# Grouped-query scores from stacked fp32r parts, decay tables behind the attentions, and a projection between MLA's transposes and products

## The chip, the cores and the metric

The kernel runs on one core of a Trainium2 chip. The metric is device time in microseconds of one execution; a run's time is the time of that core. The engines are named as the profile names them: PE (TensorE, the matmuls), PEld (its weight loads), DVE (VectorE), ACT (ScalarE), POOL (GpSimd) and SP (SyncE, which here issues most DMAs). fp32r is a 32-bit type that PE multiplies in one pass with shortened mantissas; the kernel splits an fp32 operand into a part hi and a part lo of that type and adds the products.

## The reference

One inference step of a two-layer trunk of width 1024 for 128 prompt tokens and 256 sample tokens. Each layer mixes tokens in four head groups (retention, hyena, windowed grouped-query attention, multi-head latent attention) that share one input and one output projection, and then runs a gated MLP with a short convolution. The sample's tokens read 128 cached context tokens. Cut to what matters here (GQA has 4 query heads on 2 key heads of 64, MLA 4 heads of 64+32):

```python
def rms_norm(x, g):
    xf = x.astype(jnp.float32)
    y = xf * lax.rsqrt(jnp.mean(xf * xf, axis=-1, keepdims=True) + EPS)
    return (y * g.astype(jnp.float32)).astype(x.dtype)
...
def window_attention(q, k, v, k_ctx, v_ctx, sink):
...
    valid = (jnp.abs(kpos - qpos) <= WINDOW) & (kpos >= 0) & (kpos < seq_len)
    scale = d ** -0.5
    s_win = jnp.einsum('bkgnqd,bknjd->bkgnqj', qb, kw).astype(jnp.float32) * scale
    s_win = jnp.where(valid, s_win, NEG_INF)
    s_ctx = jnp.einsum('bkgnqd,bkcd->bkgnqc', qb, k_ctx).astype(jnp.float32) * scale
...
    pr = jax.nn.softmax(jnp.concatenate([s_win, s_ctx, s_sink], axis=-1), axis=-1).astype(v.dtype)
...
def token_mixer(h, p, cache):
...
    proj = h @ p['w_in']
    ret_in, hy_in, gqa_in, mla_in = jnp.split(proj, [RET_IN, RET_IN + HY_IN, RET_IN + HY_IN + GQA_IN], axis=-1)
...
    y_ret, ret_state = retention_mixer(ret_in, p['ret_decay_logit'], p['ret_gn_g'], s0)
    y_hy = hyena_mixer(hy_in, p)
...
    mq = (rms_norm(q_lat, p['mla_q_norm']) @ p['mla_w_uq']).reshape(
        b, seq_len, MLA_HEADS, MLA_NOPE + MLA_ROPE).transpose(0, 2, 1, 3)
...
    ckv = rms_norm(kv_lat, p['mla_kv_norm'])
    if latent:
...
        o_gqa = window_attention(apply_rope(gq, cos_g, sin_g), apply_rope(gk, cos_g, sin_g), gv,
                                 cache['gqa_k'], cache['gqa_v'], sink)
...
        o_gqa = dense_attention(gq, gk, gv, HEAD_DIM ** -0.5, sink)
...
    o_mla = dense_attention(mq, mk, mv, (MLA_NOPE + MLA_ROPE) ** -0.5, None)[:, :, 0]
...
    y = jnp.concatenate([y_ret, y_hy, y_gqa, y_mla], axis=-1) @ p['w_out']
    return y, ctx_state
...
def trunk_layer(x, mod, p, cache):
    shift1, scale1, gate1, shift2, scale2, gate2 = mod
    h = rms_norm(x, p['norm_g'][0]) * (1.0 + scale1) + shift1
    y, ctx_state = token_mixer(h, p, cache)
    x = x + gate1 * rms_norm(y, p['norm_g'][1])
    h = rms_norm(x, p['norm_g'][2]) * (1.0 + scale2) + shift2
    x = x + gate2 * rms_norm(conv_ffn(h, p), p['norm_g'][3])
    return x, ctx_state
```

## The kernel before

The tokens stand transposed, 128 features on the partitions, in 386 columns: the prompt (128), and the two halves of the sample (128 each) with gap columns. The program speaks of them as u=0, 1, 2 and of their first columns as C0 = [0, 130, 258], or T0 = [0, 128, 256] where there are no gaps. Weights come from HBM in units of 512 KB into tiles raw (DMAs of SP); ACT casts a unit into whi (L358) and DVE makes wlo (L359), in halves of 512 columns. A projection of 128 features (fmps) is 24 fp32r matmuls of 386 columns: 8 blocks of 128 input features by three products, hi x hi, hi x lo, lo x hi (mm3, L383 to L385).

The mixer phase of a layer has these parts. A block with an order written out by hand for PE, DVE, ACT and SP holds the token-major projections (tma), the k projection of GQA, MLA's rotary key, norm, transposes (ckt, qlt, krps) and up-projections (ukps, uvps, uqps), and GQA's q projection u=0. The generators mla and gqa hand over at each yield, and the block says with next(ml) and next(gq) who goes on. Behind the block a scheduler decides the order from data dependencies, its own estimates and program order; there come the rest of mla (its attention), the rest of gqa (the projection u=1, gsw with the rope, its attention), hyena's six projections, and retention's.

An attention (attend, L893 to L932) does the groups u = 1, 2, 0 in turn. For one group: four heads' scores on PE into four banks, for each a maximum on DVE (L900); negm (L905); four exponentials on ACT with their sums (L908); for GQA the sink's term (L912 to L914); rc (L916); then two rounds of: P times rc (L922), six transposes ptp on PE (L925), two copies PT (L926, DVE and ACT), the products pv (L930), and a split of the result. GQA's scores before are fp32 matmuls on 64 rows (L1058, 384 columns; for the prompt L1056, 128 columns), and a bf16 matmul adds the mask (L1060). Their operands lie in one tile gqk (k in kall, q behind it); gfm tiles of the tag w15 hold the projections until the rope (gsw on PE, L1034; products on DVE and POOL, sum on DVE, L1036 to L1039) has gone into gqk.

PSUM has eight banks: two in a pool for the tag a (fmps and a few sums), five of the tag m, one n. SBUF tags are rings: the tag w15 has 11 tiles of 128 x 386, given out in program order; GQA's three gfm tiles, the six of hyena's cv (L1078 to L1080, which free a bank of fmps) and, in layer 0, the lag table and four tabt tiles of the decay tables come from it. In layer 0 the decay tables (load_lp: L540 to L560 with a chain of small operations lgp; rettab: L563 to L577) stand in the program ahead of the attentions; those of layer 1 are made in layer 0's FFN. PE also runs the adaLN projection of layer 0 in this phase (adaps, L407, four matmuls side by side) wherever its data is there.

## Time and profile before

| | before |
|---|---|
| median of 3 runs | 1088.33 us (1086.99 to 1088.36) |
| the profiled execution | 1084.69 us, of which the span shown is 1082.9 us |
| PE busy | 1059.6 us, 98% of the span |
| DVE / ACT / POOL busy | 727.2 (67%) / 504.3 (47%) / 61.5 us (6%) |
| chain that ended last | PE 86%, DVE 8%, DMA 2%, ACT 2% |
| HBM traffic | 162 GB/s over the span |

The profile is one execution. Its times run from the start of the span; layer 0's mixer lies from about 54 to 230 us, layer 1's from about 590 to 790. In rows of the time line the columns are start, duration, engine, line, operation, output and inputs with shape and type, and the number of instructions that the row joins; a bracket tells how long the engine had been idle and who released it. A matmul's duration holds its drain too, so what one costs in a series is read from the distance of two starts.

### The profile page before, as it was taken

The page shows a single profiled execution, that of the slowest core. Times are in us where ns is not written, and L with a number is a line of the kernel's source. Part 1 is how long each engine was busy: PE and PEld are TensorE (multiplying, and loading weights), DVE is VectorE, ACT ScalarE, POOL GpSimd, SP SyncE. Part 2 cuts the span into 40 slices and gives each one's busy share as a digit, 9 for nine tenths or more (in the row PEclk, how much of TensorE's full clock was granted, in tenths as well). Part 3 has the DMA queues.
Part 4 walks back from the last instruction along what each step waited for, and adds up shares of the span by engine and source line. Part 5 has one row for each costly group of instructions (what it writes and reads, how often), then busy time and mean ns, then how long its engine had stood idle before and what let it go on. Part 6 is the DMA issues. An engine that isn't in the chain of part 4 may idle for free.

```text
span 1082.9 us, 15620 instructions
## 1 busy us (share of the span) xinstructions
PE 1059.6 (98%) x5763; PEld 894.1 (83%) x5763; DVE 727.2 (67%) x1544; ACT 504.3 (47%) x1106; POOL 61.5 (6%) x74
## 2 busy tenths in 40 slices
PE   9999999999889999999999999999999999999997
PEld 4496767768789999899996977886899999999996
DVE  5868965476789885799557577757766455545544
ACT  5754635334734344333447454552584344334333
POOL 2210000000200000000002000001020000000000
PEclk9999999999999999999999999999999999999999
DMA  9674345855576764577356522231535433443301
GB/s 345 231 278 169 118 155 178 302 168 222 180 250 201 226 215 150 159 234 221 124 169 209 179 79 77 60 97 41 217 109 191 129 117 118 136 131 122 119 19 58
DMA packets 53017, 176.05 MB, mean 163 GB/s; under 512 B 8618, under 2 KB 10538, under 8 KB 52429
## 3 DMA queue, kind: packets, MB, share of 16 engines
q1 hardware_dynamic: 49229, 171.19, 47.2%
q10 hardware_dynamic: 3712, 3.87, 1.0%
q8 instruction: 45, 0.74, 0.3%
q14 instruction: 31, 0.25, 0.1%
HBM read 169.60 MB, written 5.44 MB: 162 GB/s over the span
## 4 chain that ended last, share of the span: by engine, by line
PE 86%; DVE 8%; DMA 2%; ACT 2%; issue 1%; POOL 0%; ACTq 0%; DVEq 0%; SPq 0%; POOLq 0%
PE ups L383 5%; PE ups L385 5%; PE ups L384 5%; PE gps L383 5%; PE facc L1283 5%; PE facc L1285 5%; PE gps L385 5%; PE gps L384 5%; PE facc L1284 5%; PE fmps L383 4%; PE fmps L385 4%; PE fmps L384 4%; PE adaps L407 2%; PE acc L1283 2%; PE acc L1284 2%; PE acc L1285 2%
## 5 line engine op out<-in xcount | busy, mean ns | idle before, releaser
L359 DVE TENSOR_TENSOR wlo<-raw,whi 128x512 fp32r<-128x512 f32 (+2 forms) x388 | 254.4, 686 | 169.0 <-ACT whi L358 168.5
L358 ACT CAST whi<-raw 128x512 fp32r<-128x512 f32 (+2 forms) x388 | 221.6, 611 | 276.5 <-DMA raw<-in_wdn_dram 99.1
L1283 PE MATMUL facc<-whi,fah 128*128 128x512 f32 x264 | 105.3, 399 | 2.7 <-ACT fah L358 2.7
L1285 PE MATMUL facc<-whi,fal 128*128 128x512 f32 x264 | 104.5, 397 | 0.2 <-DVE fal L359 0.2
L1284 PE MATMUL facc<-wlo,fah 128*128 128x512 f32 x264 | 104.5, 396 | 0.0
L505 DVE SCALAR_TENSOR_TENSOR avc<-avr,cs,avc 128x1024 f32<-128x1024 f32 x56 | 70.3, 1282 | 0.3 <-DMA avr<-in_ada_dram 0.2
L383 PE MATMUL gps<-hTa,whi 128*128 128x386 f32 (+4 forms) x184 | 62.5, 340 | 0.0
L383 PE MATMUL ups<-hTb,whi 128*128 128x386 f32 (+4 forms) x184 | 61.7, 335 | 0.6 <-ACT hTb L812 0.6
L384 PE MATMUL ups<-hTb,whi 128*128 128x386 f32 (+4 forms) x184 | 61.4, 334 | 0.8 <-POOL hTb L815 0.8
L385 PE MATMUL gps<-hTa,wlo 128*128 128x386 f32 (+4 forms) x184 | 62.0, 337 | 0.0
L384 PE MATMUL gps<-hTa,whi 128*128 128x386 f32 (+4 forms) x184 | 61.8, 336 | 0.0
L383 PE MATMUL gps<-hTb,whi 128*128 128x386 f32 (+4 forms) x184 | 61.7, 335 | 0.0
L383 PE MATMUL ups<-hTa,whi 128*128 128x386 f32 (+4 forms) x184 | 61.7, 335 | 0.0
L385 PE MATMUL ups<-hTb,wlo 128*128 128x386 f32 (+4 forms) x184 | 61.5, 334 | 0.0
L385 PE MATMUL gps<-hTb,wlo 128*128 128x386 f32 (+4 forms) x184 | 61.4, 334 | 0.0
L385 PE MATMUL ups<-hTa,wlo 128*128 128x386 f32 (+4 forms) x184 | 61.4, 334 | 0.0
L384 PE MATMUL ups<-hTa,whi 128*128 128x386 f32 (+4 forms) x184 | 61.3, 333 | 0.0
L384 PE MATMUL gps<-hTb,whi 128*128 128x386 f32 (+4 forms) x184 | 61.3, 333 | 0.0
L1285 PEld LDWEIGHTS facc<-whi,fal 128*128 128x128 f32 x264 | 50.0, 189 | 13.1 <-DVE fal L359 1.3
L1283 PEld LDWEIGHTS facc<-whi,fah 128*128 128x128 f32 x264 | 50.0, 189 | 13.0 <-ACT fah L358 3.0
L1284 PEld LDWEIGHTS facc<-wlo,fah 128*128 128x128 f32 x264 | 50.0, 190 | 10.1
L1299 ACT ACTIVATE fth<-fc 128x386 f32<-128x386 f32 x44 | 23.2, 528 | 59.9 <-DVE fc L1298 59.9
(381 smaller groups left out, 2371.4 us busy)
## 6 DMA issues: line engine op xcount, KB each, us to landing
raw<-in_wup_dram SPq DMA_DIRECT2D x88, 512.0 KB
araw<-in_ada_dram SPq DMA_DIRECT2D x64, 512.0 KB
raw<-in_wdn_dram SPq DMA_DIRECT2D x44, 512.0 KB
avr<-in_ada_dram SPq DMA_DIRECT2D x32, 512.0 KB
raw<-in_win_dram SPq DMA_DIRECT2D x30, 512.0 KB
raw<-in_wout_dram SPq DMA_DIRECT2D x16, 512.0 KB
gg<-gd SPq DMA_DIRECT2D x8, 512.0 KB
raw<-in_wta_dram SPq DMA_DIRECT2D x8, 416.0 KB
```

Of the source, the lines that this page charges most:

```text
L358: S.copy(hi, src)
L359: (eng or V).tensor_tensor(out=lo, in0=src, in1=hi, op=ALU.subtract)
L383: T.matmul(out, ah, bh, start=start, stop=False)
L384: T.matmul(out, ah, bl, start=False, stop=False)
L385: T.matmul(out, al, bh, start=False, stop=stop)
L407: T.matmul(self.ps[32 * j:32 * j + 32, :], cs[:, k, :], rows[j // 2][:, 512 * (j % 2):512 * (j % 2) + 512], start=(k == self.k0), stop=(k ...
L505: V.scalar_tensor_tensor(out=acc[:, v, c], in0=raw, scalar=sc, in1=acc[:, v, c], op0=ALU.mult, op1=ALU.add)
L1283: T.matmul(acc[t][h], ah[:, cs_], wh_[:, hs], start=first, stop=False)
L1284: T.matmul(acc[t][h], ah[:, cs_], wl_[:, hs], start=False, stop=False)
L1285: T.matmul(acc[t][h], al[:, cs_], wh_[:, hs], start=False, stop=last)
L1299: S.activation(out=th, in_=c, func=ACTF.Tanh)
```

## The change

Four things are edited.

1. GQA's scores. k goes into a tile gkf (tag mq, which MLA's mq uses later), and from it into kh (hi, on both halves of the rows) and kl (lo on the rows of its own head group, zeros on the other half, set by POOL). For each query head a tile gq of the tag w15 has q's hi part in 64 rows and its lo part in the other 64. One fp32r matmul of gq with kh and one with kl, on 128 rows each, take the place of the fp32 matmul. The rope is added in place in gfm or gkf, behind gsw, which reads it. The context keys stand behind the sample's now, so vals and the mask's place change. The copies L1040 go.
2. Layer 0's decay tables: load_lp is cut into the load and lp_tables; lp_tables and retention_tables of layer 0 stand in the program behind both attentions.
3. MLA yields behind its transposes, and the block with the written order puts GQA's projection u=0 between these and the up-projections; the split of its weight is written ahead of the k projection's, in tiles of its own.
4. In the FFN, the steps of the next layer's adaLN vectors (AdaV, DVE) start at f = 3, not 1.

```diff
--- before.py
+++ after.py
@@ -536,6 +536,9 @@
             o, w = poff[name]
             return t[:, o + a:o + (w if b is None else b)]
 
+        return t, get
+
+    def lp_tables(t, get):
         fh = lpp.tile([128, NF, 4], F32, tag="ffh", name="ffh")
         V.tensor_scalar(fh.rearrange("p f t -> p (f t)"), get("ffc"), 0.5, None, ALU.mult)
 
@@ -985,6 +988,7 @@
             T.transpose(ps[0:96, o:o + 128], kr[:, t, :], ident)
         for h in range(4):
             (S.copy if h % 2 else V.tensor_copy)(mk[64:96, h, 128:512], ps[64:96, 128:512])
+        yield
         wuk, wuv = M("wuk"), M("wuv")
         wuq = M("wuq").rearrange("p (k h m) -> p k h m", k=2, h=4)
         for hp in range(2):
@@ -1020,49 +1024,61 @@
 
     def gqa(l, mx, my, M, hi, lo, tma, sink, ws):
 
-        gqk = mx.tile([128, 2048], F32, tag="gqk", name="gqk")
-        kall = gqk[:, 0:512]
-        nc.sync.dma_start(out=kall[:, 0:128], in_=A["kcT"][l])
+
+        kf = my.tile([128, 514], F32, tag="mq", name="gkf")
+        gqk = mx.tile([128, 4, 514], F32R, tag="gqk", name="gqk")
+        kh, kl = gqk[:, 0:2], gqk[:, 2:4]
+        nc.sync.dma_start(out=kf[:, 386:514], in_=A["kcT"][l])
+        halfs = [slice(0, 64), slice(64, 128)]
+        for g in range(2):
+            G.memset(kl[halfs[1 - g], g].bitcast(F32), 0.0)
         yield
-        q = gqk[:, 512:1280].rearrange("p (t c) -> p t c", t=2)
+        qs = {}
         rc, rs_ = cc("rc"), cc("rs")
         for u in (2, 0, 1):
             ps = fm_mm(ws.pop(0), hi, lo) if ws else fm_proj(l, u, hi, lo)
-            fm = mx.tile([128, TP], F32, tag="w15", name="gfm", bufs=11)
-            S.activation(out=fm, in_=ps[:, 0:TP], func=ACTF.Copy, scale=1.0 if u == 2 else 0.125)
+            fm = kf if u == 2 else mx.tile([128, TP], F32, tag="w15", name="gfm", bufs=11)
+            S.activation(out=fm[:, 0:TP], in_=ps[:, 0:TP], func=ACTF.Copy, scale=1.0 if u == 2 else 0.125)
             sw = bank("m", "gsw")
             T.matmul(sw[:, 0:256], cc("perm"), fm[:, 130:386], start=True, stop=True)
-            ds_, dp = (kall[:, 128:384], kall[:, 384:512]) if u == 2 else (q[:, u, 128:384], q[:, u, 0:128])
             tmp = my.tile([128, 256], F32, tag="k1", name="grt", bufs=2)
             V.tensor_tensor(out=tmp, in0=sw[:, 0:256], in1=rs_, op=ALU.mult)
-            G.tensor_tensor(out=ds_, in0=fm[:, 130:386], in1=rc, op=ALU.mult)
-            V.tensor_tensor(out=ds_, in0=ds_, in1=tmp, op=ALU.add)
-            V.tensor_copy(dp, fm[:, 0:128])
             if u == 2:
                 pk = bank("m", "gkt")
                 T.transpose(pk[:, 0:128], fm[:, 0:128], ident)
                 ko = my.tile([128, 128], F32, tag="ko", name="ko")
                 S.copy(ko, pk[:, 0:128])
                 nc.scalar.dma_start(out=O["o_k"][l].rearrange("g t d -> t g d"), in_=ko.rearrange("t (g d) -> t g d", g=2))
+            G.tensor_tensor(out=fm[:, 130:386], in0=fm[:, 130:386], in1=rc, op=ALU.mult)
+            V.tensor_tensor(out=fm[:, 130:386], in0=fm[:, 130:386], in1=tmp, op=ALU.add)
+            for g in range(2):
+                a, b = halfs[g], halfs[1 - g]
+                if u == 2:
+                    S.copy(kh[a, g], kf[a])
+                    V.tensor_copy(kh[b, g], kf[a])
+                    V.tensor_tensor(out=kl[a, g], in0=kf[a], in1=kh[a, g], op=ALU.subtract)
+                else:
+                    q = qs[2 * g + u] = mx.tile([128, TP], F32R, tag="w15", name=f"gq{2 * g + u}", bufs=11)
+                    S.copy(q[a], fm[a])
+                    V.tensor_tensor(out=q[b], in0=fm[a], in1=q[a], op=ALU.subtract)
             yield
         nc.scalar.dma_start(out=O["o_v"][l].rearrange("g t d -> t g d"),
                             in_=tma[:, 0, 256:384].rearrange("t (g d) -> t g d", g=2))
         vc = M("vc")
         for u in (1, 2, 0):
             def score(ps, h):
-                r = 64 * (h // 2)
-                lq = q[r:r + 64, h % 2, T0[u]:T0[u] + 128]
-                if u == 0:
-                    T.matmul(ps[:, 0:128], lq, kall[r:r + 64, 384:512], start=True, stop=True)
-                else:
-                    T.matmul(ps[:, 0:384], lq, kall[r:r + 64, 0:384], start=True, stop=False)
-                    mo = 256 if u == 1 else 128
+                q, g = qs[h][:, C0[u]:C0[u] + 128], h // 2
+                k0, n = (0, 128) if u == 0 else (130, 384)
+                T.matmul(ps[:, 0:n], q, kh[:, g, k0:k0 + n], start=True, stop=False)
+                T.matmul(ps[:, 0:n], q, kl[:, g, k0:k0 + n], start=False, stop=(u == 0))
+                if u:
+                    mo = 256 - 128 * u
                     T.matmul(ps[:, mo:mo + 128], identb, maskb[:, 128 * (u - 1):128 * u], start=False, stop=True)
             def vals(k, h):
                 g = 64 * (h // 2)
                 if u == 0:
                     return tma[:, 0, 256 + g:320 + g]
-                return vc[:, g:g + 64] if k == 0 else tma[:, k, 256 + g:320 + g]
+                return vc[:, g:g + 64] if k == 2 else tma[:, 1 + k, 256 + g:320 + g]
             attend(mx, my, score, 128 if u == 0 else 384, 1.0, sink(), vals, 4, u)
 
 
@@ -1415,23 +1431,28 @@
                 wsplit(uw[0], *us[0], 0)
                 wsplit(uw[0], *us[0], 1)
                 next(ml)
+                us.append(wparts())
+                wsplit(uw[1], *us[1], 0)
+                wsplit(uw[1], *us[1], 1)
                 next(gq)
-                us.append(wparts())
-                wsplit(uw[1], *us[0], 0)
-                wsplit(uw[1], *us[0], 1)
                 next(ml)
                 next(gq)
+                next(ml)
                 end = V.tensor_copy(zero8, zero8)
             if l == 0:
                 mkf = hm.tile([128, 256], F32, tag="hm", name="mkf")
                 nc.sync.dma_start(out=mkf, in_=A["mask"])
                 with tc.issue_after(end.ins):
                     V.tensor_copy(maskb, mkf)
-                    lps = load_lp(0)
-                    rt = retention_tables(lps[2], mx, tag="w15", bufs=11)
-            get, fh, lgt = lps
+                    lp0 = load_lp(0)
+                get = lp0[1]
+            else:
+                get, fh, lgt = lps
             run(ml)
             run(gq)
+            if l == 0:
+                _, fh, lgt = lp_tables(*lp0)
+                rt = retention_tables(lgt, mx, tag="w15", bufs=11)
             hyg = hyena(l, mx, my, get, sp, hi, lo)
             reg = retention(l, mx, M, get, rt, hi, lo, tma)
             next(hyg)
@@ -1537,7 +1558,7 @@
                 act[f] = (ah, al)
                 with late if f == 0 else nullcontext():
                     wd[f] = wunit(A["wdn"][l, f], 1024, fx, STAG)
-                if f not in (0, 4, 5):
+                if f > 2 and f not in (4, 5):
                     next(nexts, None)
                     next(nexts, None)
                 if f == NF - 1:
@@ -1546,7 +1567,7 @@
                     if f == 4:
                         sp = per.tile([128, 3, 2, 512], F32, tag="spec", name="spec")
                         nc.sync.dma_start(out=sp, in_=sd[l + 1])
-                        lps = load_lp(l + 1)
+                        lps = lp_tables(*load_lp(l + 1))
                         rt = retention_tables(lps[2], av, tag="avr", bufs=2)
             run(nexts)
             avc.__exit__(None, None, None)

```

What moves is shown here as lists of instructions in an engine's order, with the tiles' numbers (they differ between the two programs).

PE, layer 1, the end of MLA's attention (its group u=0: ptp, pv) and the start of GQA's (gsw, sc); fmps are projections. Before:

```order
L385 MATMUL fmps_6868<-hTa_5483,wlo_6863 128x386
L383 MATMUL fmps_6868<-hTb_5487,whi_6862 128x386
L930 MATMUL pv_6445<-PT_6436,mv_6172 64x128 x2
L1034 MATMUL gsw_6499<-gfm_6497,cst_80 128x256
L1058 MATMUL sc_6507<-gqk_5944 128x384
L1060 LDWEIGHTS identb_94
L1060 MATMUL sc_6507<-maskb_95,identb_94 128x128
L384 MATMUL fmps_6868<-hTb_5489,whi_6862 128x386
L385 MATMUL fmps_6868<-hTb_5487,wlo_6863 128x386
```

Now:

```order
L928 MATMUL ptp_6469<-cst0_79,P_6454 128x128
L933 MATMUL pv_6472<-PT_6463,mv_6247 64x128 x2
L928 MATMUL ptp_6479<-cst0_79,P_6455 128x128
L928 MATMUL ptp_6483<-cst0_79,P_6456 128x128
L933 MATMUL pv_6486<-PT_6477,mv_6247 64x128 x2
L1043 MATMUL gsw_6540<-gfm_6538,cst_80 128x256
L1072 MATMUL sc_6553<-gqk_5974,gq0_6233 128x384
L1073 MATMUL sc_6553<-gqk_5974,gq0_6233 128x384
L1076 LDWEIGHTS identb_94
L1076 MATMUL sc_6553<-maskb_95,identb_94 128x128
L1072 MATMUL sc_6554<-gqk_5974,gq1_6546 128x384
```

No fmps stands between MLA's prompt scores and the end of GQA's first scores now; 120 stand ahead of that place in layer 1, where 157 stood, and 120 in layer 0, where 167 stood.

ACT, layer 1, the first copy cv of a hyena projection. Before, it stands between two groups of MLA's attention (P are its exponentials):

```order
L926 COPY PT_6304<-ptp_6312 128x3x128
L358 CAST whi_6862<-raw_6860 128x512 x2
L358 CAST mix_6300<-pv_6317 128x128
L1078 ACTIVATE cv_6759<-fmps_6734,lp_3537 128x386
L908 ACTIVATE P_6342,ssum_6340<-sc_6326,negm_6339 128x384
L908 ACTIVATE P_6343,ssum_6340<-sc_6327,negm_6339 128x384
```

Now, it stands behind the last group of MLA's attention and the casts of GQA's q tiles gq1 and gq3:

```order
L929 COPY PT_6463<-ptp_6469 128x128
L358 CAST mix_6341<-pv_6472 128x128
L929 COPY PT_6477<-ptp_6483 128x128
L358 CAST mix_6341<-pv_6486 128x128
L1062 CAST gq1_6546<-gfm_6538 64x386
L1062 CAST gq3_6549<-gfm_6538 64x386
L1094 ACTIVATE cv_6817<-fmps_6792,lp_3550 128x386
L1094 ACTIVATE cv_6862<-fmps_6837,lp_3550 128x386
L911 ACTIVATE P_6578,ssum_6575<-sc_6553,negm_6574 128x384
```

The first two cv have moved from MLA's attention to behind gq3. In layer 0 the two first cv follow gq3 too.

DVE, layer 0, the softmax of GQA's first group (u=1: mxv, negm, es, ssum, rc, P). Before:

```order
L900 TENSOR_REDUCE mxv_1375<-sc_1374 128x1
L359 TENSOR_TENSOR wlo_1856<-raw_1853,whi_1855 128x512
L904 TENSOR_TENSOR mxv_1375<-mxv_1375,lp_1057 128x4
L905 TENSOR_SCALAR negm_1388<-mxv_1375 128x4
L912 TENSOR_TENSOR es_1400<-lp_1057,negm_1388 128x4
L914 TENSOR_TENSOR ssum_1389<-ssum_1389,es_1400 128x4
L916 RECIPROCAL rc_1404<-ssum_1389 128x4
L922 TENSOR_SCALAR P_1392<-P_1392,rc_1404 128x384
```

Now:

```order
L903 TENSOR_REDUCE mxv_1328<-sc_1327 128x1
L573 TENSOR_SCALAR tab_1589<-lag_1585,lgt_1559 128x384
L907 TENSOR_TENSOR mxv_1328<-mxv_1328,lp_1069 128x4
L574 TENSOR_SCALAR tabt_1590<-lag_1585,nlg_1587 128x384
L908 TENSOR_SCALAR negm_1345<-mxv_1328 128x4
L573 TENSOR_SCALAR tab_1589<-lag_1585,lgt_1559 128x384
L915 TENSOR_TENSOR es_1357<-lp_1069,negm_1345 128x4
L575 TENSOR_TENSOR tab_1589<-tab_1589,tabt_1590 128x384
L574 TENSOR_SCALAR tabt_1596<-lag_1585,nlg_1587 128x384
L573 TENSOR_SCALAR tab_1589<-lag_1585,lgt_1559 128x384
L575 TENSOR_TENSOR tab_1589<-tab_1589,tabt_1596 128x384
L574 TENSOR_SCALAR tabt_1602<-lag_1585,nlg_1587 128x384
```

Operations of the decay tables (tab, tabt) stand among those of the softmax now; the tables' chains of small operations (lgp), of both layers, stand ahead of MLA's norm in layer 0.

## Rows read from the trace of the kernel before

**Rows 1.** The profile's busy times: engine, busy us, share, instructions.

```profile
PE 1059.6 (98%) x5763; PEld 894.1 (83%) x5763; DVE 727.2 (67%) x1544; ACT 504.3 (47%) x1106; POOL 61.5 (6%) x74
```

**Rows 2.** Stretches: from:to, length, busy us (instructions) of PE, PEld, DVE, ACT, POOL; clock; DMA.

```profile
637.00:670.00 33.00, 32.95 (x211) 27.78 (x211) 24.25 (x65) 17.72 (x49) 1.15 (x2) 1.00 0.21 65
```

**Rows 3.** What PE waited for from 612 to 640: total us, times, longest.

```profile
PE ukps L992 <- ACT ckvT L975: 1.0, 1, 1.0
PE uvps L998 <- ACT mv L999: 0.7, 1, 0.7
PE uvps L998 <- ACT mk L987: 0.3, 1, 0.3
```

**Rows 4.** Time line of PE, layer 1, GQA's scores of u=1.

```profile
674.15 0.91 PE L1058 MATMUL sc<-gqk 64*128 64x384 f32 x2
...
675.15 0.91 PE L1058 MATMUL sc<-gqk 64*128 64x384 f32 x2
...
676.03 0.42 PE L385 MATMUL fmps<-hTb,wlo 128*128 128x386 f32 x1
676.29 0.34 PE L383 MATMUL fmps<-hTb,whi 128*128 128x386 f32 x1
676.47 0.35 PE L384 MATMUL fmps<-hTb,whi 128*128 128x386 f32 x1
```

**Rows 5.** Time line of PE, layer 1, GQA's scores of the prompt.

```profile
699.62 0.72 PE L1056 MATMUL sc<-gqk 64*128 64x128 f32 x8
```

**Rows 6.** Time line of PE, layer 1, MLA's u=2 and u=0, then GQA's u=1.

```profile
650.20 2.85 PE L1016 MATMUL sc<-mk,mq 96*128 96x384 f32 x8
...
657.53 0.85 PE L925 MATMUL ptp<-cst,P 128*128 128x128 f32 x6
...
662.64 1.16 PE L1016 MATMUL sc<-mk,mq 96*128 96x128 f32 x8
...
667.00 0.38 PE L925 MATMUL ptp<-cst,P 128*128 128x128 f32 x2
...
670.24 0.70 PE L1034 MATMUL gsw<-gfm,cst 128*128 128x256 f32 x2
...
680.74 0.94 PE L925 MATMUL ptp<-cst,P 128*128 128x128 f32 x6
...
682.29 0.45 PE L930 MATMUL pv<-PT,lm 128*64 128x128 f32 x4 [0.25 <-ACT PT L926]
```

**Rows 7.** Time line of DVE, layer 1, the split ahead of negm.

```profile
653.56 0.68 DVE L359 TENSOR_TENSOR wlo<-raw,whi 128x512 fp32r<-128x512 f32 x1
```

**Rows 8.** Time line of PE, layer 0, from MLA's prompt scores to GQA's u=2.

```profile
136.40 1.16 PE L1016 MATMUL sc<-mk,mq 96*128 96x128 f32 x8
...
144.19 0.70 PE L1034 MATMUL gsw<-gfm,cst 128*128 128x256 f32 x2
...
155.49 1.06 PE L407 MATMUL adaps<-araw,cs 128*32 128x512 f32 x8
...
156.77 0.82 PE L925 MATMUL ptp<-cst,P 128*128 128x128 f32 x6
...
161.35 0.91 PE L1058 MATMUL sc<-gqk 64*128 64x384 f32 x2
```

**Rows 9.** Time line of DVE, layer 0's tables, and PE's wait behind them.

```profile
109.00 0.17 DVE L558 TENSOR_SCALAR lgp<-lgp 128x12 f32<-128x12 f32 x1
...
113.25 0.41 DVE L570 TENSOR_SCALAR tab<-lag,lgt 128x384 f32<-128x384 f32 x1
113.58 0.55 DVE L572 TENSOR_TENSOR tab<-tab,tabt 128x384 f32<-128x384 f32 x1
...
119.28 0.88 PE L925 MATMUL ptp<-cst,P 128*128 128x128 f32 x6 [0.78 <-DVE P L922]
```

**Rows 10.** Stretches at the end of the span, columns as in group 2.

```profile
1076.00:1080.00 4.00, 0.00 (x0) 0.00 (x0) 2.78 (x8) 0.98 (x3) 0.00 (x0) 1.00 0.20 77
...
1081.00:1082.90 1.90, 0.00 (x0) 0.00 (x0) 0.00 (x0) 0.00 (x0) 0.00 (x0) 0.50 0.13 49
```

## The prediction, before any run of the changed kernel

> **What bounds the kernel now.** I read the page's busy times first: TensorE (PE) is busy 98% of the span [rows 1], so time can only be lost or won in what PE executes and in the gaps between. Then the table by stretches: the stretch of layer 1 that holds MLA's attention has 32.95 us of PE work in 33.00 us [rows 2]. It is that full because the scheduler puts hyena projections (fmps, matmuls of 386 columns) between an attention's scores, its transposes (ptp) and its products (pv); the softmax on DVE and ACT runs beneath them. Then the waits: PE's real gaps in this part of layer 1 are three, before MLA's up-projections: 1.0, 0.7 and 0.3 us [rows 3]. So the question for each edit is not how long an operation takes on DVE or ACT, but how much PE work is left to stand beneath the chain it belongs to.
>
> **Scores.** A windowed GQA head costs 1.00 us: 674.15 to 675.15, score and mask [rows 4]. In fp32r a matmul of 386 columns follows the one before after 0.18 us, and the first one behind a bf16 mask after 0.26 us [rows 4]. A new head is an entry of 0.26, one more at 0.18 and the mask at some 0.05, so 0.5 us: four heads gain 2.0 us, and there are two such groups in each layer (u=1, u=2). The trace shows no fp32r matmul of a 64-row pair stacked to 128; bounds are 0.9 us a head (were each as slow as half an fp32 pair) and 0.4, and I take 0.5, since rows and columns are those of the fmps. The prompt's scores (u=0) were eight entries of fp32 on 128 columns in 0.72 us [rows 5]; eight fp32r ones cost at most 8 x 0.18 = 1.4 and, with a third of the columns, at least 0.5: +0.3 for each layer, between -0.2 and +0.7.
>
> **Where the fill goes.** This term decides. The four q tiles take places in the 11-buffer tag w15 that hyena's cv tiles also use, in program order: two gfm and four gq per layer, where three gfm stood. The order lists show what follows: ACT's first cv copy stands behind the casts of gq1 and gq3, and these need the last gsw, which waits behind the whole MLA attention. The projections' PSUM pool has two banks; until cv is copied out, two hyena units fill them and PE can start no third. So exactly 120 fmps (three GQA and two hyena units) stand before GQA's first score, in either layer; before, 167 stood there in layer 0 and 157 in layer 1. PE executes in order, so the stretches behind the 120th are as long as their dependency chains. The displaced fmps themselves run later at the same 0.18 us. I count, for each stretch, its length less its fill, before and after.
>
> Layer 1, first score of MLA's u=2 to first of u=0: 650.20 to 662.64 is 12.44 us [rows 6] with 33 fmps (5.9), so 6.6 uncovered. After: 11 fmps (2.0) are left. The softmax from first score to first ptp took 7.33, of which one split of a weight stood in DVE's queue right ahead of negm (0.6, [rows 7]): 6.7; two rounds of ptp, copy and pv without fill take some 4.3, worked out from ptp to pv below. 11.0 - 2.0 = 9.0: **+2.4**.
>
> MLA's u=0 to gsw: 662.64 to 670.24 is 7.60 [rows 6] with 29 fmps (5.2), 2.4 uncovered. After: no fill. Scores to ptp took 4.36 [rows 6], less some 0.4 of copies and order; two rounds on 128 columns are 2.0. 5.9 uncovered: **+3.5**.
>
> gsw to the end of the scores: 670.24 to 676.03, 5.8 with 7 fmps (1.2). After: gq1 needs gsw, two rope products, the add, a cast and a subtraction, some 2.9 us, with a reduce possibly in between, then three heads at 0.5: 4.5 to 5.3 without fill. **+0.4**; the first group's 2.0 us are spent here.
>
> GQA's u=1 softmax: 676.03 to 680.74, 4.7 [rows 4, 6], was covered by 26 fmps. After 23 are left and the scores come twice as fast as the reduces follow: **+1.0**. From ptp to pv it is 1.55 us with 0.25 idle in spite of two fmps [rows 6]; three remain. u=2 keeps 29 fmps over the same chain, so its scores' gain counts: **-1.8**. The three waits of [rows 3] go, because the u=0 projection now stands between the transposes and the up-projections and gives ACT's copies seven us: **-2.0**. With u=0's scores (+0.3) and some more changes between fp32 and fp32r (0.08 each, +0.3), layer 1 loses **4.1 us**.
>
> Layer 0: MLA's u=2 keeps its adaLN groups (adaps, 1.0 us a group, [rows 8]) as fill: 0. u=0 to gsw, 136.40 to 144.19 [rows 8], loses 23 fmps and comes down to the same 5.9 with one group and a piece: 2.7 uncovered before, 4.6 after: **+1.9**. From gsw to ptp, 144.19 to 156.77 [rows 8]: 26 fmps and three groups covered 7.6 of 12.6, 5.0 uncovered. After no fmps is left, only some 1.6 of adaps and adat. The chain is gsw to gq1 (some 4 us, as the adaLN sum stands ahead of gq1's subtraction on DVE), three heads (1.5), then the softmax. Here the moved tables hurt: of the tab operations (0.41 and 0.55 us, [rows 9]) two stand ahead of negm, seven between negm and ssum, a little more than the exponentials cover, and two ahead of P, so some 6.3 us rather than 4.7 from last score to ptp. 11.8 - 1.6 = 10.2: **+5.2**. From ptp to u=2's scores, 156.77 to 161.35, 8 fmps go, and three tab and two cv operations stand ahead of the second PT copy: 3.2 uncovered before, some 5.2 after: **+2.0**. u=2's scores -1.8, u=0's +0.3, changes of type +0.3.
>
> What the tables gain: the 0.78 us of PE at 119.28 [rows 9], where P stood behind them: -0.8. What they cost earlier: both layers' log chains, 22 operations of 0.17 us each [rows 9] and some 0.2 apart, now stand ahead of MLA's norm on DVE, and ACT loads tables twice more, once right ahead of the norm's sqrt. Much of this falls where DVE waited for PE and the constants, so I estimate 2 us of delay, of which PE feels 0.7 (0 to 1.2). Layer 0 loses **7.8 us**.
>
> DVE gets some 3.6 us and ACT 3.3 us of casts and subtractions per layer, POOL two memsets; beyond the chains above fmps or the 7 us gap stand beneath them, so 0. If that cover were gone, k's split, some 2.5 us on DVE, would delay MLA's copies. The AdaV steps of layer 0's FFN begin three units later: 34 steps are needed, 34 calls are left; DVE has the room, 0 (-1 to +1.5, as the last may run beside the end).
>
> Sum: 4.1 + 7.8 = 11.9. The profiled execution took 1084.69 us (span 1082.9, and 1.8 around it), 3.6 below the median; a like execution would be 1096.6, and the median of the shown runs, 1088.33, becomes **1100 us**.
>
> The Trainium skill, "Perfetto Trace Analysis", section Identifying Performance Opportunities, reads a repeated gap on the engine that should be saturated as a possible lack of buffers for the next tile. Before, the row of [rows 2] shows no such gap; by that rule the change makes one, which agrees with the ring above and adds nothing to the sum.
>
> **Rivals.** (a) Faster: the gaps close, because with no hyena work between them DVE and ACT answer at once, and the scores' gain is left. It needs the softmax chains to shrink to what fill remains. For it: PE's 98% leave the new scores' 8 us and the 2.0 of [rows 3] as clear gains. Against: the chain from u=1's last mask to ptp is 4.7 us of operations nearly end to end, with one split in it. The price: -7.2 for scores, +0.6 for u=0, -2.8 for waits gone, with the gaps at 0 to 2: 1079 to 1082.
>
> (b) Half: chains about 30% shorter than I composed, 6 us less: 1091 to 1096. For it: each chain carries splits and copies in the trace that leave it when the fill does.
>
> (c) The clock. Behind the last matmul (1076.0) the granted clock stayed 1.00 to 1080 and was 0.50 in the last 1.9 us [rows 10]: it fell some 4.5 us after PE stopped. Layer 0's new gap between GQA's u=1 scores and ptp is some 5 us. If the clock falls there to its lower level, the matmuls behind run at half speed until it rises; at 2 to 6 us of PE work, that is +2 to +6: 1102 to 1108. This decides if the gap outlasts what the tail shows. The Trainium skill, "TensorE: Matmul & The Clock Gate", Part 1, says likewise that an idle array is throttled from 2.4 to 1.2 GHz; the tail agrees, and no run here shows it inside the attention.
>
> (d) The change doesn't do what it says: the new scores' subtraction chain holds up every head, so fp32r gains nothing: +4 us, 1104.
>
> **How the numbers follow.** Forecast 1100, with 1095 to 1107 for its own bounds (the chains' +-30%, the unknown prices): 0.62. (a) 0.12, (b) 0.12, (c) above 1104 and (d) together 0.10, and 0.04 for no change. The range reaches from (b) to (c) and (d): 1090 to 1110. About 0.2% (2 us) is what a measurement of this kernel can tell from no change. Faster 0.12, same 0.04, slower 0.84.
>
> **What would show it.** In the profile after: new PE gaps of some 9 us in layer 1 and 12 in layer 0 (the net losses plus the scores' gain and the waits gone), in the attentions, released by DVE's P and ACT's PT and gq; ACT's first cv right behind gq3; heads at 0.5 us; no wait at ukps and uvps; 143 fmps in one piece behind layer 1's attention; a clock of 1.00. It is wrong if PE stays over 98% busy there, if heads cost 0.8, or if the new time lies in the FFN.

## The result, and the profile after

| | before | changed |
|---|---|---|
| median of 4 runs | 1087.66 us (1084.87 to 1088.36) | 1114.34 us (1112.07 to 1114.70) |
| ratio, 95% interval | | 1.0246 [1.0223, 1.0269] |
| span of the profiled execution | 1082.9 us | 1112.9 us |

The changed kernel is slower by 26.7 us; the two profiled executions lie 30.0 us apart. The forecast was 1100 with a range to 1110, so the direction came true and the size did not. The two profiled executions differ by more than the medians; part of that lies in the execution, as told further down.

The page's busy times of the changed kernel (engine, busy us, share of the span, instructions):

```profile
PE 1068.0 (96%) x5763; PEld 906.7 (81%) x5763; DVE 735.6 (66%) x1554; ACT 513.7 (46%) x1120; POOL 65.9 (6%) x78
```

PE was 98% busy before [rows 1] and is 96% busy now. It also has more busy time than before, though its scores got cheaper: part of its work ran slower. Where it stands still, the table of PE's waits over the whole span tells (line, the releaser, us in total, times, longest):

```profile
PE ptp L928 <- DVE P L925: 12.5, 5, 5.6
PE sc L1072 <- DVE gq L1063: 3.8, 2, 2.2
...
PE gsw L1043 <- ACT gfm L1041: 1.6, 2, 0.8
PE fmps L383 <- DVE mxv L907: 1.3, 1, 1.3
PE pv L933 <- DVE PT L929: 1.3, 5, 0.3
```

The two at the top are the attentions': PE waits for the softmax (P) and for GQA's q tiles. The table by stretches shows where (us from the start, length, busy us of PE, PEld, DVE, ACT, POOL with instructions, granted clock, DMA share, GB/s); these two answer to [rows 2]:

```profile
640.00:673.00 33.00, 30.40 (x148) 22.49 (x148) 22.36 (x50) 15.81 (x40) 0.64 (x1) 1.00 0.25 80
673.00:710.00 37.00, 28.57 (x160) 22.15 (x161) 23.16 (x65) 14.23 (x43) 0.64 (x1) 0.77 0.10 30
```

In the second, PE idles 8.4 of 37 us, and its granted clock is 0.77. PE's time line of that part in the changed kernel (start, duration, operation, count, and in brackets the idle time ahead and its releaser) answers to [rows 6]:

```profile
674.20 1.27 PE L928 MATMUL ptp<-cst,P 128*128 128x128 f32 x6 [2.06 <-DVE P L925]
...
679.97 1.16 PE L1020 MATMUL sc<-mk,mq 96*128 96x128 f32 x8
684.00 0.49 PE L928 MATMUL ptp<-cst,P 128*128 128x128 f32 x2 [2.88 <-DVE P L925]
...
687.18 1.22 PE L1043 MATMUL gsw<-gfm,cst 128*128 128x256 f32 x2
...
691.39 0.66 PE L1072 MATMUL sc<-gqk,gq 128*128 128x384 f32 x1 [2.21 <-DVE gq L1063]
...
695.53 0.66 PE L383 MATMUL fmps<-hTa,whi 128*128 128x386 f32 x1 [1.27 <-DVE mxv L907]
```

From the last fmps ahead of 674.20, at 671.79, to the one at 695.53 PE executes not one projection. Before, 29 matmuls of them lay between u=0's scores and gsw, and 33 from there to GQA's transposes; now there are none and 23, these all behind 695.53. ACT's time line of the changed kernel has the reason:

```profile
690.14 1.05 ACT L1062 CAST gq<-gfm 64x386 fp32r<-64x386 f32 x2 [2.58 <-DVE gfm L1053]
691.21 1.24 ACT L1094 ACTIVATE cv<-fmps,lp 128x386 f32<-128x386 f32 x2
```

The first cv, which frees a bank of fmps, stands right behind the casts of GQA's q tiles, and those wait for a gsw that waits for all of MLA's attention. In layer 0 the first cv follows them too, and there operations of the decay tables ([rows 9] has them before) lie in the gap as well. PE's time line and, below it, DVE's, in layer 0 of the changed kernel:

```profile
147.05 0.42 PE L1072 MATMUL sc<-gqk,gq 128*128 128x384 f32 x1
...
147.52 0.42 PE L1072 MATMUL sc<-gqk,gq 128*128 128x384 f32 x1
...
154.22 1.12 PE L928 MATMUL ptp<-cst,P 128*128 128x128 f32 x4 [5.59 <-DVE P L925]
```

```profile
150.19 0.16 DVE L908 TENSOR_SCALAR negm<-mxv 128x4 f32<-128x4 f32 x1
150.27 0.41 DVE L573 TENSOR_SCALAR tab<-lag,lgt 128x384 f32<-128x384 f32 x1
...
152.59 0.41 DVE L573 TENSOR_SCALAR tab<-lag,lgt 128x384 f32<-128x384 f32 x1
152.93 0.16 DVE L917 TENSOR_TENSOR ssum<-ssum,es 128x4 f32<-128x4 f32 x1
```

A head now takes 0.47 us from start to start, against 1.00 before [rows 4]. The table operations fill DVE from negm to ssum, and PE stands 5.59 us.

### The profile page after: what moved, and what is told of

The parts are those of the page before. It is cut to its first block, busy times and chain, and to the rows that moved or that the text cites. A ratio compares the mean times of both kernels' runs of the same rounds, so it can differ in the third digit from the quotient of the medians.

```text
span 1112.9 us, 15674 instructions
## 1 busy us (share of the span) xinstructions
PE 1068.0 (96%) x5763; PEld 906.7 (81%) x5763; DVE 735.6 (66%) x1554; ACT 513.7 (46%) x1120; POOL 65.9 (6%) x78
## 4 chain that ended last, share of the span: by engine, by line
PE 87%; DVE 7%; ACT 3%; DMA 2%; issue 1%; POOL 0%; DVEq 0%; SPq 0%; ACTq 0%; POOLq 0%
PE facc L1299 6%; PE gps L383 5%; PE facc L1301 5%; PE facc L1300 5%; PE ups L383 5%; PE ups L385 5%; PE gps L385 5%; PE ups L384 5%; PE gps L384 5%; PE fmps L383 3%; PE fmps L385 3%; PE fmps L384 3%; PE adaps L407 2%; PE acc L1299 2%; PE acc L1300 2%; PE acc L1301 2%
```

## The experiments

Three groups, each timed beside runs of the kernel before on its own chip (medians 1085.81, 1085.84 and 1084.97 us). So an experiment is compared with another of the same group by medians, and across groups by the ratio to before.

### Is it the ring, and what does the clock add?

**e1_ring.** The change as it is, but gq1 and gq3 have a tag of their own, and w15 gives up two tiles for it. Nothing else is edited, and with 9 and 2 the tiles are eleven as before, so it undoes only the claimed cause.

```diff
-q = qs[2 * g + u] = mx.tile([128, TP], F32R, tag="w15", ..., bufs=11)
+q = qs[2 * g + u] = mx.tile([128, TP], F32R, tag="gqq" if u else "w15", ..., bufs=2 if u else 9)
 (all other tiles of w15: bufs=11 -> bufs=9)
```

> The changed kernel, with two q tiles (gq1, gq3) in a tag of their own and the tag w15 cut from 11 to 9 tiles to make room; nothing else. Theory R (the ring takes the fill away): the hyena copies no longer stand behind gq3, projections stand in the attentions again, and nearly all of the 26.7 us goes: 1078 to 1088, TensorE's waits for P and gq under 2 us, clock 1.00 in the attentions. Rival W (the added casts, the moved tables and the new waits for gsw cost by themselves, with or without fill): 1100 or more, with waits for P and gq still there.

1081.96 us, 0.9956 of before [0.9934, 0.9977]: the loss is gone, and a gain is left. 161 projections in layer 0 and 167 in layer 1 stand ahead of GQA's first score, where the change has 120, and PE's waits for P come to 1.4 us in all, with none for gq. ACT's time line of this kernel has a cv ahead of the casts of gq in layer 1:

```profile
665.34 0.67 ACT L1094 ACTIVATE cv<-fmps,lp 128x386 f32<-128x386 f32 x1
...
672.60 1.05 ACT L1062 CAST gq<-gfm 64x386 fp32r<-64x386 f32 x2
```

The table by stretches of this kernel, its two stretches that answer to those above:

```profile
637.00:670.00 33.00, 32.20 (x208) 27.19 (x207) 24.46 (x67) 17.30 (x48) 0.00 (x0) 1.00 0.15 49
670.00:707.00 37.00, 35.61 (x240) 30.92 (x238) 27.74 (x73) 22.63 (x62) 3.51 (x5) 1.00 0.26 86
```

In the second PE has 240 matmuls in place of 160, 35.6 of 37 us busy, at a clock of 1.00. Which ring two tiles come from decides over 2.9% of the kernel.

**e2_warm.** The change, with idle bf16 matmuls in PE's gaps: 73 in layer 0 and 66 in layer 1 (PE has 5902 matmuls in place of 5763). The 61 that the expectation names for layer 0 are those ahead of transposes; 12 more stand ahead of its second GQA score. What they write is overwritten; nothing is left out. They cost no chain anything if the gaps are real, and they are meant to hold the clock up.

```diff
 (ahead of an attention's first transposes)
+for _ in range(fill.get((k0, u), 0) if h == 0 else 0):
+    T.matmul(tp..., identb, maskb, start=True, stop=True)
 (ahead of the second GQA score of u=1)
+for _ in range((12, 18)[l] if u == 1 and h == 1 else 0):
+    T.matmul(ps[:, 0:256], identb, maskb, start=True, stop=True)
```

> The changed kernel with idle bf16 matmuls of 256 columns (identity by mask, results overwritten) put into the gaps of both attentions, each set shorter than the gap that the trace shows there: 61 in layer 0, 66 in layer 1. Theory C (the lower clock in those stretches costs on top of the gaps): the granted clock stays near 1.00 and the time falls by 5 to 9 us, to 1105 to 1109, with the chains of DVE and ACT as long as they were. Rival N (the clock falls where TensorE waits anyway, so it costs little): 1113 to 1118, the idle matmuls that are not hidden being added.

1108.95 us, 1.0215 [1.0186, 1.0244]. The granted clock by stretches, first of the changed kernel, then of this one:

```profile
148.00:154.00 6.00, 0.63 (x6) 0.39 (x5) 5.68 (x20) 3.55 (x12) 0.00 (x0) 0.85 0.61 208
154.00:158.00 4.00, 3.58 (x19) 2.72 (x20) 4.00 (x12) 2.21 (x6) 0.00 (x0) 0.50 0.02 5
672.00:674.00 2.00, 0.14 (x1) 0.00 (x0) 0.55 (x3) 2.00 (x8) 0.00 (x0) 1.00 0.00 0
674.00:676.00 2.00, 1.70 (x8) 1.17 (x8) 1.84 (x6) 0.89 (x2) 0.00 (x0) 0.62 0.00 0
...
688.00:695.00 7.00, 4.05 (x13) 2.38 (x12) 4.86 (x10) 2.26 (x4) 0.64 (x1) 0.50 0.00 0
695.00:698.00 3.00, 2.47 (x8) 2.50 (x9) 2.55 (x10) 1.85 (x7) 0.00 (x0) 0.50 0.00 0
```

```profile
148.00:154.00 6.00, 5.99 (x52) 4.73 (x53) 5.96 (x21) 3.54 (x12) 0.00 (x0) 1.00 0.00 0
154.00:158.00 4.00, 3.65 (x38) 2.39 (x32) 3.98 (x11) 3.15 (x8) 0.00 (x0) 1.00 0.49 181
...
684.00:695.00 11.00, 9.75 (x65) 8.11 (x65) 8.29 (x25) 5.30 (x16) 0.64 (x1) 1.00 0.00 1
```

In the stretches behind the gaps the clock is 0.50 to 0.62 in the changed kernel; with idle matmuls in the gap it is 1.00. What that is worth in layer 1 is read from its first gsw to hyena's first matmul (hyR), with the same projections between. PE's time line, first of the changed kernel, then of this one:

```profile
632.46 0.70 PE L1043 MATMUL gsw<-gkf,cst 128*128 128x256 f32 x2 [0.51 <-ACT gkf L1041]
...
753.23 0.59 PE L1118 MATMUL hyR<-ut,cst 128*128 128x256 f32 x2
```

```profile
631.87 0.70 PE L1047 MATMUL gsw<-gkf,cst 128*128 128x256 f32 x2 [0.51 <-ACT gkf L1045]
...
747.85 0.59 PE L1124 MATMUL hyR<-ut,cst 128*128 128x256 f32 x2
```

It is 120.77 us in the changed kernel and 115.98 here: 4.8 us of clock in that layer. In layer 0 the stretch from GQA's gsw to its u=2 scores is 1.7 us shorter (16.0 against 17.8), but the FFN begins no earlier (first gate product at 295.5 against 295.1 us): PE then waits 1.45 us for a cv of DVE, which it doesn't in the changed kernel, and behind shorter waits that hold no idle matmuls the clock is 0.50 here too (141 to 144 us). The whole kernel gains 3.4 us by the two ratios (1.0215 and 1.0246, with intervals that overlap) and 5.6 against e12, the change measured again. The rest of the loss stays, and that is right: idle matmuls are no projections.

### Which edit carries the loss?

**e3_tables_back.** The change with layer 0's tables ahead of the attentions again.

```diff
+lps = lp0[1], *lp_tables(*lp0)[1:]
+rt = retention_tables(lps[2], mx, tag="w15", bufs=11)
 ...
-if l == 0:
-    _, fh, lgt = lp_tables(*lp0)
-    rt = retention_tables(lgt, mx, tag="w15", bufs=11)
```

> The changed kernel with layer 0's decay tables back in their old place, ahead of both attentions. Theory T (the tables among GQA's softmax and the log chains ahead of MLA's norm cost layer 0 some 4 to 6 us): 1108 to 1110, with the 5.6 us wait for P in layer 0 down to some 3. Theory R alone: the tables only lengthen a gap that is there anyway, and in the old place they hold fill of their own: 1112 to 1116.

1115.54 us, 1.0279 [1.0253, 1.0304]: not faster than the change. PE's wait of 5.59 for P goes, but others come: 4.2 us for the data of adaps (a DMA) and 1.8 for its sum on DVE. The tables only stood in a gap that something fills anyway.

**e4_no_yield.** The change without the hand-over between MLA's copies and its products, so with the block's old order there.

```diff
-yield    (behind the copies of mk)
 (the block: next(gq); wparts and two wsplit of u=0; next(ml); next(gq), as before)
```

> The changed kernel without the projection between MLA's transposes and products (the old order of that block). If that edit saves the waits at the up-projections, as predicted: 2 us slower in layer 1 for the waits, +1 to +3 in all, 1115 to 1117. Rival: the edit uses up fill that the attentions lack afterwards, so undoing it is worth 3 to 7 us: 1107 to 1111.

1111.89 us, 1.0246 [1.0217, 1.0276]. A wait of 2.6 at ukps for ckvT comes back in layer 1, and the time does not rise. By itself that is inconclusive. In the traces PE's waits for P in layer 1 come to 3.2 us here, against 4.9 in the changed kernel, and layer 0's FFN begins 1.8 us earlier; what makes each of them was not separated.

**e5_scores_only.** The first edit alone: e3 and e4 together, and the AdaV steps where they were.

```diff
 (e3 and e4 together)
-if f > 2 and f not in (4, 5):
+if f not in (0, 4, 5):
```

> The kernel before with the new scores alone: q tiles in the full ring w15, while the tables, MLA's order and the FFN steps are as before. Theory R (the ring of the scores' edit makes the loss): 120 projections stand ahead of GQA's first score here too, so 1108 to 1117, the waits for P and gq as in the changed kernel. Rival (the other three edits make a good part of it): 1090 to 1100.

1109.12 us, 1.0211 [1.0182, 1.024], with 120 projections ahead of GQA's scores in both layers. The new q tiles alone bring 2.1 of the 2.5%; the other edits are not needed for the loss and do not cure it.

**e11_adav_back** and **e12_control.** The change with only the start of layer 0's AdaV steps put back, and the change unaltered beside it.

```diff
-if f > 2 and f not in (4, 5):
+if f not in (0, 4, 5):
```

> The changed kernel with the FFN steps starting at f = 1 again, the ring as in the change. If the 3.2 us between e1 and e8 are this edit's price at the end of layer 0's FFN, independent of the ring: 2 to 4 us under the control run of the same call. If it was chance or belonged to e1's alignment: within 1.5 us of it.

> The changed kernel once more, unaltered, as a control on the chip of these runs. All theories: 1.022 to 1.027 of before, so 1110 to 1115.

1110.23 us, 1.0236 [1.0209, 1.0262], and 1113.88 us, 1.0267 [1.0237, 1.0297]: 3.65 us apart, with intervals that overlap. From layer 0's first gate product to layer 1's first gsw it is 336.0 us in e11's trace and 338.7 in e12's: 2.7 us lie in this one stretch. All the traces agree on it: 336.4 to 338.7 us in the seven kernels whose steps start late, 332.9 to 336.0 in the seven where they start as before, 2.6 us between the means. The time line shows how. DVE's first yn of the layer's closing norm, in the changed kernel, in e1 and in e8 (below, where the steps are back):

```profile
579.65 1.29 DVE L774 TENSOR_TENSOR yn<-facc,gg 128x512 f32<-128x512 f32 x2 [5.26 <-DMA gg<-gd]
```

```profile
563.81 1.29 DVE L774 TENSOR_TENSOR yn<-facc,gg 128x512 f32<-128x512 f32 x2 [5.88 <-DMA gg<-gd]
```

```profile
557.32 0.69 DVE L774 TENSOR_TENSOR yn<-facc,gg 128x512 f32<-128x512 f32 x1 [1.47 <-ACT sqj L746]
```

Steps that begin two units later (f = 3, not 1) end two units later, the gate tile gg that they produce comes back by a DMA, and DVE waits 5 to 6 us for it between the layers. Where the steps start as before, that wait is not there, in e11 neither.

### What is each edit worth when the ring is free?

All of these have e1's ring, except e9, which has no new q tiles.

**e6_ring_scores_only**: e5 with e1's ring. **e7_ring_tables_back**: e1 with e3's tables. **e8_ring_adav_back**: e1 with AdaV's old start:

```diff
 (e1's ring)
-if f > 2 and f not in (4, 5):
+if f not in (0, 4, 5):
```

> The kernel before with the new scores alone and gq1, gq3 in a tag of their own (w15 with 9 tiles). By the score groups of the traces (1.8 us gained in each of four, 0.3 lost in two) 6 to 7 us faster than before: 1079 to 1081. If the casts and subtractions on DVE and ACT give part of it back, 1083 to 1086. Against e1 it tells what the other three edits are worth together once the fill is there: 0 to 3 us either way.

> As e1_ring, with the decay tables of layer 0 back ahead of the attentions. If the moved tables gain the 0.8 us wait at the first ptp and a little more, as the run e3 hints: 1083 to 1086, slower than e1 by 1 to 3 us. If their place doesn't matter under fill: within 1 us of e1.

> As e1_ring, with the FFN steps of the next layer's vectors starting at f = 1 again. The prediction priced this edit at nothing (-1 to +1.5): within 1 us of e1. If the later start leaves steps to the end of layer 0's FFN, where the clock dipped, then 1 to 2 us faster than e1.

| | median us | ratio to before, 95% |
|---|---|---|
| e6: scores alone | 1084.91 | 0.9989 [0.9971, 1.0008] |
| e7: all but the tables | 1088.67 | 1.0020 [1.0003, 1.0037] |
| e8: all but AdaV's start | 1078.73 | 0.9923 [0.9898, 0.9948] |

e6 came out as its second expectation has it, e7 and e8 outside theirs: by the ratios e7 is slower than e1 by 0.64% (the tables' place, 7 us), e8 faster by 0.33% (AdaV's start, 3.6 us). e8 is the fastest kernel of this study, 7.1 us below before. The page's busy times of e8:

```profile
PE 1050.5 (98%) x5763; PEld 895.4 (83%) x5763; DVE 735.2 (68%) x1554; ACT 512.9 (48%) x1120; POOL 65.3 (6%) x78
```

PE has 9.1 us less work than before [rows 1] at the same share. But the scores alone (e6) give only 0.9 of that, which its interval does not tell apart from nothing. PE's waits in e6, layer 0's mixer, and then layer 1's:

```profile
PE adaps L407 <- DMA araw<-in_ada_dram: 2.2, 1, 2.2
PE fmps L383 <- ACT gfm L1040: 1.5, 1, 1.5
```

```profile
PE ukps L995 <- ACT ckvT L978: 2.6, 1, 2.6
```

New casts of k stand on ACT ahead of ckvT, so the ukps wait grows from 1.0 [rows 3] to 2.6. And PE arrives at an adaLN group whose data has not landed; in e7 too (PE's waits in layer 0's mixer):

```profile
PE adaps L407 <- DMA araw<-in_ada_dram: 2.7, 1, 2.7
```

The tables' old place is not all that it takes: e10 (below), with the tables moved, has 1.7 us of this wait, while before and e9, with the old scores, have none. In e7's time line the projections that stand behind that group begin only after it, and the first ones follow each other at 0.32 us (122.99, 123.31, 123.63), not at 0.18. In e7 layer 0 also has 12.0 us from MLA's first transposes to its u=2 scores, against 5.1 in e1.

**e9_no_scores**: the kernel before, with the tables' move and the hand-over alone. **e10_ring_adav_yield_back**: e8 without the hand-over (e4's diff on e8).

```diff
 (e9, on the kernel before: the tables behind the attentions, and)
+yield    (behind the copies of mk)
```

> The kernel before with the moved tables and the projection between MLA's transposes and products, but with the old scores and the old start of the FFN steps. Against e8 (1078.7), which has the new scores beside, it tells what the scores are worth with their fill: by the score groups of the traces 6 to 7 us, so 1084 to 1086 here; if casts and subtractions give most of it back, 1079 to 1081, and the gain of e8 over before is the tables' and the projection's.

> As e8 (free ring, old FFN steps), with MLA's block in the old order. The prediction gave the projection there 2.0 us in layer 1: then 1080 to 1082. If the waits that it removes come back as others in the same block (layer 1's stretch from gsw to MLA's second scores was as long as before in the changed kernel), within 1 us of e8.

1085.60 us, 1.0002 [0.9988, 1.0016], and 1082.48 us, 0.9975 [0.9959, 0.9991]. Against e8's ratio the scores are worth 0.8% (e9), and the hand-over 0.5% (e10). In PE's waits of e10, layer 1, the three of [rows 3] stand again, two of them larger than before:

```profile
PE ukps L995 <- ACT ckvT L978: 2.6, 1, 2.6
...
PE uvps L1001 <- ACT mk L990: 0.9, 1, 0.9
PE uvps L1001 <- ACT mv L1002: 0.7, 1, 0.7
```

So the edits are not additive: scores alone 0.1%, tables and hand-over alone nothing, all three 0.8%. The scores' casts lengthen the wait at ukps that the hand-over takes away; what makes the wait for the adaLN data is not shown.

## Why the prediction was wrong

What failed, in the prediction's own terms: it kept the clock out of its sum, as a rival that decides only in a gap longer than the tail's 4.5 us; it took 2.0 us off for the three waits and counted hyena, AdaV's start and the end of the kernel as 0. The gaps themselves, its main term, it had nearly right.

Each stretch of the forecast, measured as it was forecast, in the two profiled executions: its length less its number of fmps times 0.178 us and, in layer 0, less its adaLN matmuls (adaps) at the forecast's 1.0 us for eight; changed less before. A stretch ends at the first score or matmul of what it names.

| stretch | forecast | measured |
|---|---|---|
| layer 1: first gsw to MLA's u=2 scores (the three waits and the types) | -1.7 | +0.1 |
| u=2 to u=0 | +2.4 | +4.1 |
| u=0 to gsw | +3.5 | +4.8 |
| gsw to GQA's first transposes | +1.4 | +5.1 |
| on to u=0's scores | -1.5 | -1.7 |
| layer 1, sum | +4.1 | +12.4 |
| layer 0: start to gsw, and on to MLA's u=2 | -0.1 | +0.5 |
| u=2 to u=0 | 0 | +1.1 |
| u=0 to gsw | +1.9 | +3.2 |
| gsw to GQA's first transposes | +5.2 | +4.6 |
| transposes to u=2's scores | +2.0 | +3.3 |
| on to u=0's scores | -1.5 | -2.1 |
| the rest, hyena and retention, to the FFN | 0 | +2.4 |
| layer 0, sum (with the types +0.3) | +7.8 | +13.0 |
| layer 0's FFN / layer 1's end | 0 / 0 | +1.5 / +3.1 |
| all | +11.9 | +30.0 |

**The mechanism was right.** 120 projections stand ahead of GQA's first score, the first cv follows gq3, and e1 shows that the ring decides. A head costs 0.47 us, forecast 0.5. The Trainium skill, "Perfetto Trace Analysis", section Identifying Performance Opportunities, takes a gap that repeats on the engine that should be saturated as a possible sign of too few buffers for the next tile, as the forecast cited. e1 agrees that the buffers decide, and shows one thing more: their number is the same there, only two of them are no longer in the shared ring.

**The gaps were sized nearly right.** In the stretch 635 to 710 PE idles 11.1 us now, and in 76 to 235 14.5; before it was 0.3 in layer 1 (632 to 705) and 2.0 in layer 0 (76 to 235). That is 10.8 and 12.5 more, where the forecast named 9 and 12. With the clock held (e2), layer 1's stretches from u=2 to u=0, on to gsw, and on to GQA's u=2 scores lose 3.1, 4.0 and 2.1 us, where the forecast had 2.4, 3.5 and 1.4.

**The clock was taken as a rival, and it is a term.** It was written down for layer 0's gap alone, at a small chance, with the tail's 4.5 us [rows 10] as the point from which it decides, at a price of 1102 to 1108 (1100 and its own 2 to 6 us give 1106). It fell in both layers, in layer 1 behind a gap of 2.06 us that followed four microseconds of unbroken PE work. The trace of before had the warning, outside the attentions. Two of its PE gaps, in layer 0's FFN and ahead of layer 1's, and the granted clock behind them:

```profile
306.09 0.79 PE L1283 MATMUL facc<-whi,fah 128*128 128x512 f32 x1 [2.72 <-ACT fah L358]
...
793.71 1.90 PE L799 MATMUL tps<-cst,xn 128*128 128x128 f32 x8 [1.96 <-DVE xn L792]
```

```profile
306.00:310.00 4.00, 3.91 (x11) 3.16 (x12) 4.00 (x8) 2.13 (x5) 0.00 (x0) 0.62 0.49 137
...
793.50:798.00 4.50, 4.29 (x25) 4.33 (x25) 1.43 (x5) 3.06 (x8) 2.22 (x2) 0.62 0.01 4
```

The tail shows how long the clock lasted once; it is no bound for a gap elsewhere. The clock adds to the gaps and does not replace them: 4.8 us in layer 1 by e2, and 1.7 in layer 0's stretch from gsw to u=2's scores, which e2 does not keep to the end of the layer.

**AdaV's later start was priced at 0 (-1 to +1.5) and cost some 2.6** (the means over the traces; 3.65 us by the medians of e12 and e11). The step asked whether DVE had room and whether calls were left, and did not follow the result: gg travels through a DMA and is wanted at the layer's closing norm. Its 34 calls for 34 steps leave none over, so the last step stands in the layer's last unit; and the start is two units later, not three. The table's +1.5 for this stretch compares one execution with one.

**The -2.0 for the three waits was not seen.** In the changed kernel two of them are gone and mv's is 0.3, but gsw's waits for gfm and gkf, and others, stand in their place (0.8, 0.5 and 0.3). The sum was taken against the waits of before, and the first edit changes those. From layer 1's first gsw to hyR the hand-over gives 1.4 us with the old scores (107.0 in e9, 108.4 before), with the tables' move beside it, and 3.3 with the new ones and the ring free (105.4 in e8, 108.7 in e10), where the wait would otherwise have become 2.6. Over the whole kernel e8 and e10 are 0.5% apart.

**Hyena in layer 0 was counted as 0.** Its projections stand behind the attentions now, and PE waits twice 0.8 us for Y (DVE and POOL) at hyP, waits that the trace of before doesn't have.

**Layer 1's end varies from execution to execution.** All of the +3.1 lies behind the FFN's first gate product: 292.7 us before, 295.8 in the changed kernel. But the changed kernel measured again (e12) takes 294.2, e8 295.8 and e10 292.2. PE is equally busy before, in the changed kernel and in e12 (13.04 of the first 15 us); what differs is the granted clock there: 0.89, 0.66 and 0.77. So the medians, 26.7 us apart, are the better measure of the change. What makes the clock stay down for longer in one execution is not settled.

**The sum of what is known.** Between 11.9 and 30.0 lie 18.1 us: 4.8 and 1.7 of clock, 1.8 for the waits, 2.4 for hyena in layer 0, 1.5 in layer 0's FFN and 3.1 in layer 1's end. The 2.8 that are left are spread over the chains. As the clock's part comes from another pair of kernels, this is an estimate.

**Rival (a)** named 1079 to 1082, and e1 measured 1081.96. That is chance: (a) is worked out from 1088.33, e1's own before was 1085.81, and the gain is 3.9 us where (a) had 6 to 9. Nor is it (a) that came true: its gaps were to close while the projections were away, and e1 brings the projections back. The price of the scores and the waits without gaps agrees with e8, which gains 7.1.

Left open: how the tables and the hand-over share e9's zero (in its trace layer 1 gains the 1.4 us above, and layer 0's FFN begins 0.8 later), and whether a third PSUM bank for fmps would do what e1's ring does; neither was tried by itself.

## What to carry to other kernels

A new tile that is written late, put in a ring that also serves the copies which free PSUM, stops all work behind it in program order: look at the ring's other users before the tile's cost, and give a late tile its own tag, even out of the same number of tiles. Where an engine is 98% busy, price an edit by the fill that it leaves under each chain, add the clock for each new gap (and look in the trace for the shortest gap behind which it fell already), and price edits together where one lengthens the queue that another empties. When side work is started later, follow it to its last reader, through its DMA.

## What the runs showed of the hardware

- The clock fell right behind a gap of 2.06 us in PE's work, in e7 behind one of 2.67, and in the kernel before behind gaps of 2.72 and 1.96, while at the end of the kernel it had stayed 1.00 for some 4.5 us [rows 10]. At 0.50, fmps follow each other at 0.32 us (696.31, 696.63, 696.95) where they do at 0.18 otherwise. The Trainium skill, "TensorE: Matmul & The Clock Gate", Part 1, says that the throttled rate is the default and activity releases it; e2 agrees, where idle matmuls kept the clock at 1.00 in the gaps that they fill and made layer 1's part 4.8 us shorter.
- An fp32r head on 128 rows (two matmuls of 384 columns and a bf16 mask) costs 0.47 us; at the lower clock 0.88 (692.26 to 693.14).
- A single group of adaLN matmuls that waits for a DMA held up PE for 2.2 and 2.7 us (e6, e7); in e7 projections stand behind it.
